# A hybrid decoder layer on one core: sums by another queue, weight tiles split in halves, the first keys' weights loaded early, small casts on VectorE

## The chip, the core and the metric

The kernel runs on one core of one Trainium2 chip. The metric is the device time of one execution in microseconds (us); less is better. TensorE (PE in the rows) does the matmuls, VectorE (DVE), ScalarE (ACT) and GpSimd (POOL) the rest, and SyncE (SP) issues most of the transfers between HBM and the on-chip memory. ScalarE and GpSimd have queues from which transfers are issued too.

## The reference

One layer over 576 tokens: a prompt of 512, and 8 sample sequences of 8 tokens with the same weights. All is float32.

```python
proj = x @ w_in                                   # u | q latent | kv latent | rotary key
y_ssm, h_last = s5_group(u, h0, p)                # complex diagonal scan, gelu, g * sigmoid(g @ w_glu)
q = (rms_norm(cq) @ w_uq); q_rope = rope(q[..., 128:])
q_lat = einsum(q[..., :128], w_uk)                # 8 heads; latent keys and values
o_lat = attend(q_lat, q_rope, ckv, krope)         # prompt: causal; sample: paged cache of 1024 + 8
y_att = einsum(o_lat, w_uv)
x = layer_norm(ALPHA*x + concat([y_ssm, y_att]) @ w_out)
x = layer_norm(ALPHA*x + (silu(x @ w_gate) * (x @ w_up)) @ w_down)
```

The model width is 2048, the feed-forward width 5632. The outputs are both `y`, the new kv latent and rotary key rows, and the last S5 states.

## The kernel before, in words

Every product keeps float32 accuracy by three matmuls: an operand is split into a high part `hi` (ScalarE copies it into the rounded type) and a low part `lo = raw - hi` (VectorE), and TensorE adds hi*hi, hi*lo and lo*hi. Weights are split on the chip too, so each weight tile costs a transfer, a ScalarE copy and a VectorE subtraction before TensorE can use all of it. Tokens go in two halves of 288 (`HALF`).

All engine instructions are recorded at one line (L181, the method that a planner's `Clock` wraps round every engine), so the tiles name the work: `wraw`, `whi`, `wlo` are a weight tile as it landed and its two parts; `mm` and `sc` are PSUM tiles; `xh/xl`, `Ah/Al`, `z`, `g`, `T` operands; `m` and `QS` also staging or sums.

The work is written as generators that yield until a time or a condition. `Layer.drive` and `merge` step them with the planner's estimated times (`nc.ready(tile)` is when it thinks a tile will be there), and the order in which they issue sets each engine's order, which a scheduler with priorities (`tc.cur_priority`) then refines. On the chip every engine runs its list in order and waits on semaphores.

The places that matter here:

- `Ring` holds a stream of weight tiles with two raw buffers and two split pairs. `dma` issues a load, `split` emits the ScalarE copy and the VectorE subtraction. `weights()` builds the ring of 1024 columns that serves `w_kv`, `w_uq`, `w_ukt`, `w_glu`, `w_out` and the first tiles of `w_gu`. The ring that serves `w_dn` in the feed-forward part has 1024 columns as well.
- `to_heads` ends the in-projection and starts the attention part. The wide tiles of the in-projection's weights (`wraw` 128x2048) and of the first queries' are freed there, and the ring's first two tiles, both halves of `w_kv[0]`, take their place.
- `queries`, `keys`, `qlats`, `values`, `score`, `attend` run head pairs of the prompt. `sides` runs beside them. GpSimd copies the sample tokens' columns of each query and of the latent into `qns`, `qrs` and `ckn` (40 small copies), and `sides` ends with transposes of `ckn` into `cnh`, `cnl`, for which it claims a PSUM tile twice.
- `gates` adds `g` halves on GpSimd (16 adds of 128x288).
- `ffn_phase` runs a seven-product (Strassen-like) form. `gate_up` leaves its results in HBM (`hd`), and the down product reads them back as 128x288 blocks. `ahead` lists the blocks, `loads` takes a free staging buffer (`xres` twice, `mraw`, `hraw`, and after `widen` seven pieces of `QS`, a tile that the last `gate_up` result is stored from), loads, copies to `hi`, subtracts to `lo`. `down` runs three chunks of the feed-forward width (c = 0, 1, 2). For each block of output columns it makes partial sums S (7 blocks of 288 columns, about 1 MB) that ScalarE evicts from PSUM into `m` (one buffer) or, in the last chunk, `m` and `QS` in turn; S leaves for HBM: `pa` in chunk 0 by SP's queue (8 stores), added onto `pa` by GpSimd's queue (10), `pb` by SP's queue (4, last chunk). `combine` reads them back.

The lines printed below are the functions that the diff touches.

Of the kernel before, what the change touches and what calls it, by code (L numbers as in the profile page):

```python
# [8 lines left out]
F32 = mybir.dt.float32  # L9
# [3 lines left out]
OP = mybir.AluOpType  # L13
# [6 lines left out]
TP = 512  # L20
# [318 lines left out]
class Ring:  # L339
# [31 lines left out]
    def split(self, j):  # L371
        while self.ns <= j < len(self.items):
# [12 lines left out]
            if self.split_fn:  # L385
                self.split_fn(hi, lo, raw, k)
            else:
                s = slice(0, math.prod(self.items[k].shape[1:]))
                tc = self.L.tc
                at = tc.cur_priority  # L390
                tc.cur_priority = at + 200
                self.L.split(hi[:, s], lo[:, s], raw[:, s])
                tc.cur_priority = at + 2
# [125 lines left out]
class Layer:  # L519
# [228 lines left out]
    def weights(self):  # L748
# [16 lines left out]
        for n in range(2 * HEADS):  # L765
            items += [io['w_gu'][n // 2, n % 2, 2 * r:2 * r + 2, :, :512].rearrange("q p c -> p q c") for r in range(2)]
        self.ring = Ring(self, self.wst, "w", 1024, items, ahead=100)

# [225 lines left out]
    def to_heads(self):  # L994

        nc = self.nc
        self.qns = self.mid2.tile([128, H, 2, TS], F32R, name="qns")
        self.qrs = self.mid2.tile([128, NB, 2, H, NS], F32R, name="qrs")
        self.QS = self.mid2.tile([128, 4, NB, H, NS], F32, name="QS")
        self.cn = (self.mid2.tile([64, 512], F32R, name="cnh"), self.mid2.tile([64, 512], F32R, name="cnl"))  # L1000
        self.ckn = self.mid2.tile([128, 4, 2, TS], F32R, name="ckn")
        self.QR, self.QN = {}, {}

        def main():
            w = yield from self.w_first.take()
            yield from self.rope_queries(0, *(x[:, 1024:] for x in w))
            yield from self.nope_queries(0, *w)

        self.mm_bufs = 4
        self.drive((main(), 1), *self.rest)  # L1010
        self.mm_bufs = 2
# [11 lines left out]
    def nope_queries(self, pr, wh, wl):  # L1023
        nc, p = self.nc, self.a0
        for hh in range(2):
# [11 lines left out]
            for i, x in enumerate((a, b)):  # L1037
                nc.gpsimd.tensor_copy(self.qns[:, h, i], x[:, TP:].bitcast(F32))
            self.QN[h] = (a, b)
# [9 lines left out]
            for i, x in enumerate((a, b)):  # L1049
                nc.gpsimd.tensor_copy(self.qrs[:, :, i, h],  # L1050
                                      x[:, TP:].rearrange("p (b s) -> p b s", b=NB).bitcast(F32))
# [416 lines left out]
    def prompt_phase(self):  # L1468
# [153 lines left out]
        def sides():  # L1622
# [4 lines left out]
            for i in range(4):  # L1627
                for j in range(2):
                    nc.gpsimd.tensor_copy(self.ckn[:, i, j], self.ckv[i][j][:, TP:].bitcast(F32))
            yield from qlats(0)  # L1630
            for pr in range(1, 4):
# [3 lines left out]
                yield from qlats(pr)  # L1635
                yield from values(pr)
            for j in range(2):
                ps = yield from self.claim()
                pt = ps[:64, 0]
                for i in range(4):  # L1640
                    nc.tensor.transpose(pt[:, i * 128:(i + 1) * 128], self.ckn[:, i, j].bitcast(F32), self.ident)
                nc.scalar.activation(self.cn[j], pt, AF.Copy)
                self.release(ps)
            done[0] = True
# [55 lines left out]
    def gates(self):  # L1700

        nc = self.nc
        for m in range(8):
# [3 lines left out]
            for hf in range(2):  # L1707
                nc.gpsimd.tensor_tensor(t[:, hf], g[0][hf].bitcast(F32), g[1][hf].bitcast(F32), OP.add)
            yield self.when(sg, t)
# [545 lines left out]
    def ffn_phase(self):  # L2255
# [38 lines left out]
        def loads(todo):  # L2294

            while True:
# [14 lines left out]
                nc.sync.dma_start(raw, src)  # L2311
                yield self.when(raw)
                nc.scalar.activation(hi, raw, AF.Copy)
# [73 lines left out]
        def down():  # L2387
            for c, n in enumerate(CHUNKS):
                for i in range(n2):
# [10 lines left out]
                    if c == len(CHUNKS) - 1 and i >= n2 // 2:  # L2400
                        nc.sync.dma_start(self.pb[i], S)
                    elif c:
                        nc.gpsimd.dma_start(self.pa[i], S, accum_op=OP.add)
                    else:
                        nc.sync.dma_start(self.pa[i], S)

# [100 lines left out]
```

## Time and profile before

| | |
|---|---|
| time, median of 3 runs | 2414.77 us (2414.47 to 2416.0) |
| the profiled execution: time | 2418.4 us |
| the profiled execution: span from first to last instruction | 2416.3 us |
| TensorE busy | 2316.1 us, 96% of the span, 17220 matmuls |
| VectorE busy | 1919.0 us, 79% |
| ScalarE busy | 1094.6 us, 45% |
| GpSimd busy | 48.8 us, 2% |
| mean granted TensorE clock | 0.982 |

The page gives busy time by engine. Since TensorE is busy nearly all the time, what counts is the rest: the stretches in which it waits and what ends each wait, and those in which its granted clock is below 1. A matmul of 288 columns starts every 0.13 us in a full stretch and every 0.24 us at the lower clock, so "busy" is longer than the work where the clock is down; the count of matmuls in a window of 20 us (150 or so in a full one) tells more.

### The profile page before, as it was taken

What the parts mean: (1) busy time and instruction counts of PE and PEld (TensorE: products, weight loads), DVE (VectorE), ACT (ScalarE), POOL (GpSimd) and SP (SyncE); (2) the same over time, 40 slices, a digit from 0 to 9 for tenths busy, and PEclk for the clock granted to TensorE, in tenths of its full rate; (3) what the DMA queues carried; (4) which work ended last, traced back from release to release, by engine and by line L of the source; (5) the groups of instructions that cost most, each with busy time, mean ns of one, the idle gap of its engine ahead of it and who ended that gap; (6) DMA issues with size and microseconds to landing.
All of it is one profiled execution on the core that took longest, in us unless ns stands there. A gap on an engine that the chain in (4) does not pass through costs nothing.

```text
span 2416.3 us, 44739 instructions
## 1 busy us (share of the span) xinstructions
PE 2316.1 (96%) x17220; PEld 2270.1 (94%) x17220; DVE 1919.0 (79%) x3465; ACT 1094.6 (45%) x1718; POOL 48.8 (2%) x93
## 2 busy tenths in 40 slices
PE   8999899999898999999999999999998999989996
PEld 8989799998798989999999999999998999989996
DVE  6898576778888896999988888887788776675878
ACT  4332565556555554333333333333335564464134
POOL 0000100110000000000000000000000000000000
PEclk9999899999999999999999999999999999999998
DMA  7663645678765565555433333332336665587722
GB/s 265 191 190 103 174 149 162 198 242 295 232 210 169 192 210 191 179 179 192 154 116 134 116 118 134 116 121 104 106 116 191 242 217 144 151 240 244 291 97 79
DMA packets 219352, 419.89 MB, mean 174 GB/s; under 512 B 62402, under 2 KB 127298, under 8 KB 217346
## 3 DMA queue, kind: packets, MB, share of 16 engines
q1 hardware_dynamic: 187346, 359.66, 44.8%
q10 hardware_dynamic: 30064, 44.98, 5.3%
q0 software_dynamic: 1728, 12.39, 2.8%
q8 instruction: 135, 2.21, 0.4%
q14 instruction: 79, 0.65, 0.1%
HBM read 337.52 MB, written 83.64 MB: 174 GB/s over the span
## 4 chain that ended last, share of the span: by engine, by line
PE 71%; DMA 11%; DVE 11%; ACT 4%; issue 3%; SPq 1%; ACTq 0%; DVEq 0%
PE mm L181 46%; PE sc L181 23%; DVE wlo L181 3%; DMA cktraw<-ckt 2%; ACT whi L181 1%; DMA xres<-hd 1%; PE po L181 1%; DMA wraw<-w_gu 1%; DMA wraw<-w_out 1%; DMA hd<-m 1%; DVE z L181 1%; DVE g L181 1%; DMA mraw<-so 1%; DVE E L181 1%; DVE QS L181 1%
## 5 line engine op out<-in xcount | busy, mean ns | idle before, releaser
L181 PE MATMUL mm<-xh,whi 128*128 128x288 f32 x2272 | 602.0, 301 | 18.7 <-ACT whi L181 8.8
L181 PE MATMUL mm<-xh,wlo 128*128 128x288 f32 x2272 | 602.0, 301 | 5.1 <-DVE wlo L181 4.9
L181 PE MATMUL mm<-xl,whi 128*128 128x288 f32 x2272 | 600.2, 300 | 0.9 <-DVE xl L181 0.9
L181 PEld LDWEIGHTS mm<-xh,whi 128*128 128x128 f32 x2272 | 404.7, 190 | 29.6 <-ACT whi L181 11.5
L181 PEld LDWEIGHTS mm<-xh,wlo 128*128 128x128 f32 x2272 | 404.8, 190 | 11.5 <-DVE wlo L181 8.5
L181 PEld LDWEIGHTS mm<-xl,whi 128*128 128x128 f32 x2272 | 404.9, 190 | 3.7 <-DVE xl L181 1.5
L181 PE MATMUL sc<-z,whi 128*128 128x288 f32 x1470 | 350.2, 297 | 0.0
L181 ACT ACTIVATE whi<-wraw 128x1024 fp32r<-128x1024 f32 (+2 forms) x159 | 174.0, 1095 | 276.6 <-PE mm L181 173.8
L181 ACT ACTIVATE whi<-E 128x1024 fp32r<-128x1024 f32 x120 | 127.1, 1059 | 331.4 <-issue 197.3
L181 DVE TENSOR_TENSOR wlo<-wraw,whi 128x1024 fp32r<-128x1024 f32 (+2 forms) x159 | 201.6, 1269 | 68.5 <-ACT whi L181 68.0
L181 PEld LDWEIGHTS sc<-z,whi 128*128 128x128 f32 x1470 | 250.8, 189 | 0.3 <-ACT whi L181 0.3
L181 ACT ACTIVATE whi<-rp 128x1024 fp32r<-128x1024 f32 x120 | 127.5, 1062 | 254.2 <-issue 195.2
L181 DVE TENSOR_TENSOR wlo<-E,whi 128x1024 fp32r<-128x1024 f32 x120 | 146.8, 1223 | 95.6 <-ACT whi L181 94.8
L181 PE MATMUL mm<-T,H 128*128 128x288 f32 x1200 | 216.1, 295 | 0.0
L181 DVE TENSOR_TENSOR wlo<-rp,whi 128x1024 fp32r<-128x1024 f32 x120 | 146.6, 1222 | 70.7 <-ACT whi L181 70.3
L181 PEld LDWEIGHTS mm<-T,H 128*128 128x128 f32 x1200 | 179.8, 188 | 0.0
L181 PE MATMUL sc<-Ah,H 128*128 128x288 f32 x552 | 145.4, 299 | 11.7 <-ACT m L181 9.9
L181 PE MATMUL sc<-g,whi 128*128 128x288 f32 x490 | 144.6, 295 | 2.1 <-ACT g L181 1.9
L181 PE MATMUL sc<-z,wlo 128*128 128x288 f32 x490 | 145.9, 298 | 0.5 <-DVE wlo L181 0.5
L181 PE MATMUL sc<-g,wlo 128*128 128x288 f32 x490 | 144.5, 295 | 0.0
L181 PE MATMUL mm<-Ah,H 128*128 128x288 f32 x552 | 144.2, 297 | 0.0
L181 PE MATMUL mm<-Ah,whi 128*128 128x288 f32 x480 | 134.0, 301 | 6.1 <-ACT whi L181 3.4
(488 smaller groups left out, 4930.3 us busy)
## 6 DMA issues: line engine op xcount, KB each, us to landing
wraw<-w_gu SPq DMA_DIRECT2D x145, 512.0 KB, 3.3
qns<-w_gu SPq DMA_DIRECT2D x59, 512.0 KB, 3.3
wraw<-w_out SPq DMA_DIRECT2D x56, 512.0 KB, 4.0
wraw<-w_dq SPq DMA_DIRECT2D x43, 512.0 KB, 4.4
cktraw<-ckt SPq DMA_DIRECT2D x64, 320.0 KB, 4.4
cknraw<-ckn SPq DMA_DIRECT2D x64, 256.0 KB, 4.3
hd<-QS ACTq DMA_DIRECT2D x16, 1008.0 KB, 6.3
wraw<-w_in SPq DMA_DIRECT2D x14, 1024.0 KB, 4.9
```

What stands on the lines that cost most here:

```text
L181: r = f(*a, **k)
```

## The change

Six things change:

- `Ring.split`: for a ring of 1024 columns, two copies and two subtractions of 512 columns each take the place of one of 1024.
- `to_heads` allocates the tile `QS` early (as `self.kv`, 128x2048), loads all of `w_kv[0]` into it in one transfer at a raised priority, and `weights` hands its halves to the ring as items 0 and 1. The real `QS` takes the buffer later, in `sides`.
- The 40 small copies and the 16 adds go from GpSimd to VectorE.
- `sides` claims one PSUM tile for both transposes of `ckn`, not two one after the other.
- `loads` of the feed-forward part plans the ScalarE copy of a block 1.5 us later than the planner's time of landing. This is no wait on the chip; it moves the copy, and what follows from it, in the order of the engines.
- `down` issues its `pa` and `pb` stores from ScalarE's queue; those that add onto `pa` stay on GpSimd's.

```diff
@@ Ring.split
-                self.L.split(hi[:, s], lo[:, s], raw[:, s])
+                n = s.stop // 2 if self.n == 1024 else s.stop
+                for i in range(0, s.stop, n):
+                    self.L.split(hi[:, i:i + n], lo[:, i:i + n], raw[:, i:i + n])
@@ weights
-        self.ring = Ring(self, self.wst, "w", 1024, items, ahead=100)
+        ring = self.ring = Ring(self, self.wst, "w", 1024, items, ahead=100)
+        ring.raw, ring.nd = {i: self.kv[:, 1024 * (1 - i):1024 * (2 - i)] for i in range(2)}, 2
@@ to_heads
-        self.QS = self.mid2.tile([128, 4, NB, H, NS], F32, name="QS")
+        self.kv = self.mid2.tile([128, 2048], F32, name="QS")
+        at = self.tc.cur_priority
+        self.tc.cur_priority = max(at - 400, 0)
+        nc.sync.dma_start(self.kv, self.io['w_kv'][0])
+        self.tc.cur_priority = at
@@ nope_queries, rope queries
-                nc.gpsimd.tensor_copy(self.qns[:, h, i], x[:, TP:].bitcast(F32))
+                nc.vector.tensor_copy(self.qns[:, h, i], x[:, TP:].bitcast(F32))
-                nc.gpsimd.tensor_copy(self.qrs[:, :, i, h],
+                nc.vector.tensor_copy(self.qrs[:, :, i, h],
@@ sides
-                    nc.gpsimd.tensor_copy(self.ckn[:, i, j], self.ckv[i][j][:, TP:].bitcast(F32))
+                    nc.vector.tensor_copy(self.ckn[:, i, j], self.ckv[i][j][:, TP:].bitcast(F32))
+            self.QS = self.mid2.tile([128, 4, NB, H, NS], F32, name="QS")
...
+            ps = yield from self.claim()
             for j in range(2):
-                ps = yield from self.claim()
-                pt = ps[:64, 0]
+                pt = ps[:64, j]
...
-                self.release(ps)
+            self.release(ps)
@@ gates
-                nc.gpsimd.tensor_tensor(t[:, hf], g[0][hf].bitcast(F32), g[1][hf].bitcast(F32), OP.add)
+                nc.vector.tensor_tensor(t[:, hf], g[0][hf].bitcast(F32), g[1][hf].bitcast(F32), OP.add)
@@ ffn_phase, loads
-                yield self.when(raw)
+                yield ('t', nc.ready(raw) + 1500)
@@ ffn_phase, down
-                        nc.sync.dma_start(self.pb[i], S)
+                        nc.scalar.dma_start(self.pb[i], S)
...
-                        nc.sync.dma_start(self.pa[i], S)
+                        nc.scalar.dma_start(self.pa[i], S)
```

**The start of the attention part, SP.** SP's transfers at the end of the in-projection before (`Sd<-hst` gathers S5 states, `U`, `M`, `P` belong to the S5 blocks):

```order
L181 DMA wraw<-w_uq 128x1536
L181 DMA Sd<-hst 64x8x63 x2
L181 DMA o_sp<-so 128x64
L181 DMA Sd<-hst 64x8x63 x13
L181 DMA wraw<-w_kv 128x1024 x2
L181 DMA Sd<-hst 64x8x63
L181 DMA U<-us_60 128x576
```

and now:

```order
L181 DMA wraw<-w_uq 128x1536
L181 DMA Sd<-hst 64x8x63 x2
L181 DMA o_sp<-so 128x64
L181 DMA Sd<-hst 64x8x63 x5
L181 DMA QS<-w_kv 128x2048
L181 DMA Sd<-hst 64x8x63 x5
L181 DMA wraw<-w_ukt 128x1024
L181 DMA wraw<-w_uq 128x512
L181 DMA Sd<-hst 64x8x63 x4
L181 DMA U<-us_60 128x576
```

The load of the first keys' weights stands ahead of nine of the state transfers that it stood behind, and two more weight loads stand before the last four.

**The same place, ScalarE**, before (`qnh`, `qrh`, `kr`, `rt` belong to the first queries and keys, `lsq` to a norm, `hst` to the S5 states):

```order
L181 ACTIVATE lsq<-mm 32x576 x4
L181 ACTIVATE hst<-S 128x1008
L181 ACTIVATE rt<-mm 32x576 x4
L181 ACTIVATE qnh<-mm 128x576
L181 ACTIVATE kr<-rva 128x576
L181 DMA o_kr<-rva 64x576
L181 ACTIVATE qnh<-mm 128x576
L181 ACTIVATE qrh<-qr 64x576 x4
L181 ACTIVATE whi<-wraw 128x1024 x2
```

and now:

```order
L181 ACTIVATE lsq<-mm 32x576 x4
L181 ACTIVATE qnh<-mm 128x576
L181 ACTIVATE rt<-mm 32x576 x4
L181 ACTIVATE hst<-S 128x1008
L181 ACTIVATE whi<-QS 128x512 x4
L181 ACTIVATE qnh<-mm 128x576
L181 ACTIVATE kr<-rva 128x576
L181 DMA o_kr<-rva 64x576
L181 ACTIVATE qrh<-qr 64x576 x4
```

The copies of the keys' weights, now four of 512 columns, stand ahead of one `qnh`, of `kr` and of the four `qrh`.

**The first blocks of the down product, ScalarE**, from the operand block `xh1` to the second eviction, before:

```order
L181 ACTIVATE xh1_193<-mraw_22285 128x288
L181 ACTIVATE xh1_193<-hraw_22292 128x288
L181 ACTIVATE T40_11236<-xres_22334 128x288
L181 ACTIVATE Ah4_10019<-xres_22340 128x288
L181 ACTIVATE Ah4_10019<-mraw_22343 128x288
L181 ACTIVATE whi_22206<-E_22198 128x1024
L181 ACTIVATE Ah12_5553<-hraw_22350 128x288
L181 DMA hd21_138<-QS_12323 128x1152
L181 ACTIVATE H_22202<-qns_22059 128x768
L181 ACTIVATE m_22196<-sc_22197 128x288
L181 ACTIVATE m_22196<-mm_22218 128x576
```

and now, from the first eviction on:

```order
L181 DMA hd21_138<-QS_12548 128x1152
L181 ACTIVATE H_22423<-qns_22284 128x768
L181 ACTIVATE m_22417<-sc_22418 128x288
L181 ACTIVATE xh6_198<-xres_22656 128x288
L181 ACTIVATE xh6_198<-xres_22659 128x288
L181 ACTIVATE xh3_195<-mraw_22824 128x288
L181 ACTIVATE xh1_193<-QS_22511 128x288 x2
L181 ACTIVATE z01_11811<-QS_22511 128x288 x2
L181 ACTIVATE g1_11720<-QS_22511 128x288
L181 ACTIVATE m_22417<-mm_22441 128x576
```

The block `xh1` comes now from pieces of `QS`, behind the store of `hd21` that reads `QS` and behind the first eviction, where it came from `mraw` and `hraw` ahead of both.

**The same place, TensorE**, before, from the products with `xh1`:

```order
L181 MATMUL mm_22218<-xh1_193,whi_22136 128x288
L181 MATMUL mm_22218<-xl1_209,whi_22136 128x288
L181 MATMUL mm_22218<-xh1_193,wlo_22137 128x288
L181 MATMUL mm_22218<-xh1_193,whi_22136 128x288
L181 MATMUL mm_22218<-xl1_209,whi_22136 128x288
L181 MATMUL mm_22218<-xh1_193,wlo_22137 128x288
L181 MATMUL mm_22265<-xh4_196,whi_22075 128x288
```

and now:

```order
L181 MATMUL mm_22482<-T40_11402,H_22296 128x288 x2
L181 MATMUL mm_22482<-T40_11402,H_22297 128x288
L181 MATMUL sc_22636<-Ah0_10040,H_22423 128x288
L181 MATMUL sc_22636<-Al0_10041,H_22423 128x288
L181 MATMUL sc_22636<-Ah0_10040,H_22424 128x288
L181 MATMUL sc_22636<-Ah0_10040,H_22423 128x288
L181 MATMUL sc_22636<-Al0_10041,H_22423 128x288
L181 MATMUL sc_22636<-Ah0_10040,H_22424 128x288
L181 MATMUL mm_22441<-xh1_193,whi_22359 128x288
L181 MATMUL sc_22456<-z01_11811,whi_22359 128x288
L181 MATMUL mm_22441<-xl1_209,whi_22359 128x288
```

The products with `xh1` stand now behind those of `xh4` and `T40` and behind the first product of the next output block (`sc_22636`); they stood ahead of all three.

## Rows read from the trace of the kernel before

**Rows 1.** The page, busy time, share and instructions of each engine.

```profile
PE 2316.1 (96%) x17220; PEld 2270.1 (94%) x17220; DVE 1919.0 (79%) x3465; ACT 1094.6 (45%) x1718; POOL 48.8 (2%) x93
```

**Rows 2.** TensorE's waits: engine, tile, releaser, us in total, times, longest.

```profile
PE mm L181 <- ACT whi L181: 23.0, 13, 10.8
PE sc L181 <- ACT m L181: 10.7, 6, 4.1
PE mm L181 <- DVE wlo L181: 8.6, 14, 1.1
```

**Rows 3.** TensorE, timeline at the first keys: start, us, instruction [idle before <-releaser].

```profile
281.08 0.58 PE L181 MATMUL mm<-whi,xh 128*128 128x256 f32 x1 [10.84 <-ACT whi L181]
282.65 0.79 PE L181 MATMUL mm<-xh,whi 128*128 128x512 f32 x1 [0.99 <-ACT whi L181]
```

**Rows 4.** SP's queue, timeline at the first keys.

```profile
258.67 15.01 SPq L181 DMA_DIRECT2D Sd<-hst  x13
273.78 1.13 SPq L181 DMA_DIRECT2D wraw<-w_kv  x2
```

**Rows 5.** ScalarE, timeline at the first keys.

```profile
266.77 2.61 ACT L181 ACTIVATE lsq<-mm 32x576 f32<-32x576 f32 x4
269.40 1.99 ACT L181 ACTIVATE hst<-S 128x1008 f32<-128x1008 f32 x1
...
274.05 0.65 ACT L181 ACTIVATE qnh<-mm 128x576 fp32r<-128x576 f32 x1
...
279.97 1.06 ACT L181 ACTIVATE whi<-wraw 128x1024 fp32r<-128x1024 f32 x1 [1.00 <-DMA wraw<-w_kv]
```

**Rows 6.** Weight splits by shape, ScalarE and VectorE: xcount | busy, mean ns | idle before.

```profile
L181 ACT ACTIVATE whi<-wraw 128x1024 fp32r<-128x1024 f32 x129 | 136.1, 1057 | 193.9 <-PE mm L181 105.5 <-DMA wraw<-w_gu 29.3 <-DMA wraw<-w_out 24.5
L181 ACT ACTIVATE whi<-wraw 128x512 fp32r<-128x512 f32 x15 | 9.5, 632 | 5.1 <-DMA wraw<-w_in 4.3 <-PE mm L181 0.6
...
L181 DVE TENSOR_TENSOR wlo<-wraw,whi 128x1024 fp32r<-128x1024 f32 x129 | 157.6, 1222 | 50.2 <-ACT whi L181 49.6
L181 DVE TENSOR_TENSOR wlo<-wraw,whi 128x512 fp32r<-128x512 f32 x15 | 10.2, 688 | 6.3 <-ACT whi L181 6.3
```

**Rows 7.** TensorE, timeline, two waits on one ring tile.

```profile
741.71 0.40 PE L181 MATMUL mm<-xh,whi 128*128 128x288 f32 x1 [1.06 <-ACT whi L181]
743.32 0.40 PE L181 MATMUL mm<-xh,wlo 128*128 128x288 f32 x1 [0.64 <-DVE wlo L181]
```

**Rows 8.** Windows of 20 us: busy time (instructions) of each engine, granted clock, DMA share, GB/s.

```profile
440.00:460.00 20.00, 17.65 (x119) 16.80 (x118) 16.66 (x42) 13.34 (x32) 0.00 (x0) 0.91 0.51 138
...
860.00:880.00 20.00, 16.53 (x116) 15.35 (x114) 20.00 (x31) 11.06 (x18) 0.00 (x0) 1.00 0.79 252
```

**Rows 9.** TensorE, timeline, the wait behind the transposes of `ckn`.

```profile
442.65 0.63 PE L181 MATMUL mm<-c,ckn 128*64 128x128 f32 x4 [2.35 <-ACT cnh L181]
```

**Rows 10.** VectorE, groups by shape: two like the added copies and adds.

```profile
L181 DVE TENSOR_TENSOR m<-m,sc 128x288 f32<-128x288 f32 x22 | 9.8, 448 | 0.0
L181 DVE TENSOR_TENSOR xl<-tmu,xh 128x64 fp32r<-128x64 f32 x8 | 1.4, 218 | 0.0
```

**Rows 11.** TensorE, timeline, waits in the down product.

```profile
1856.91 0.61 PE L181 MATMUL sc<-Ah,H 128*128 128x288 f32 x1 [4.05 <-ACT m L181]
...
1863.07 0.40 PE L181 MATMUL sc<-g,whi 128*128 128x288 f32 x1 [1.75 <-ACT g L181]
...
2173.00 0.40 PE L181 MATMUL sc<-Ah,H 128*128 128x288 f32 x1 [1.52 <-ACT H L181]
...
2247.28 0.40 PE L181 MATMUL mm<-xh,whi 128*128 128x288 f32 x1 [1.88 <-ACT whi L181]
```

**Rows 12.** ScalarE, timeline in the down product.

```profile
1860.32 0.94 ACT L181 ACTIVATE z<-QS 128x288 fp32r<-128x288 f32 x2 [0.89 <-DMA QS<-hd]
...
1870.63 0.63 ACT L181 ACTIVATE m<-mm 128x576 f32<-128x576 f32 x1
```

**Rows 13.** SP's queue, timeline in the down product.

```profile
1871.29 0.32 SPq L181 DMA_DIRECT2D pa<-m  x1
```

## The prediction, made before the changed kernel had run

> **What bounds the kernel now.** I read the page's busy shares first. TensorE is busy 2316.1 of 2416.3 us, and VectorE, the next, 1919.0 [rows 1]. So a change pays where TensorE waits or where its clock is down, and only there. The list of TensorE's waits comes next [rows 2]: 23.0 us in 13 waits for the high part of a weight tile, 8.6 us in 14 waits for the low part, 10.7 us in 6 waits for an eviction into `m`. The reader is to see that the biggest sum has one large member, 10.8 us. Then the timeline at each large wait, to see what was late, and the windows round it, to see what else was full.
>
> **The first keys.** TensorE stops at 270.24 (281.08 less 10.84) and starts at 281.08, does one matmul and waits 0.99 more before 282.65 [rows 3]. What is late is the transfer: SP issues thirteen `Sd<-hst` over 15.01 us and `w_kv` only at 273.78 [rows 4]; ScalarE copies it at 279.97 after 1.00 us of waiting for it [rows 5]. In the new order the load stands behind seven `Sd` transfers in all, two of them ahead of the stretch in the rows, so about a third into it, near 264; even if it takes twice what the two 0.5 MB loads took (273.78 to 279.97, 6.2 us), it lands at 276.4, and at the old pace near 270. ScalarE then decides. Its list ahead of the first copy is the four `lsq`, which end at 269.38, one `qnh`, the four `rt` and `hst`. The same work less one `qnh` and plus `kr` and a `qnh` ran before from 269.40 to 274.70 [rows 5], so the first new copy can start near 274.7 less 0.7, or 274.0. A copy of 512 columns takes 0.63, its subtraction 0.69 [rows 6]; TensorE now wants both, so it restarts at 275.4 at the earliest, and at 277 if VectorE's list or the landing is late. Idle time was 10.84 + 0.99 = 11.8 and is then 5.2 to 6.8, and no second wait follows, since three more copies of 0.63 keep ahead of 24 matmuls on each. The gain is 5.0 to 6.6; I take **5.5**, for the range 3 to 7 (3 if the transfer shares the engines badly). The `Sd` transfers that are passed, and the two loads put before the last four, delay the S5 blocks' state loads; the new order of TensorE has S5's products later too, which is the second rival's place.
>
> **Weight tiles in halves.** 129 tiles of 1024 columns are split at 1.057 us of ScalarE and 1.222 of VectorE; 15 of 512 columns at 0.632 and 0.688 [rows 6]. Where TensorE waits for a tile, the first half's high part is there 1.057 - 0.632 = 0.43 earlier, and its low part at 0.632 + 0.688 = 1.32 instead of 1.057 + 1.222 = 2.28, so 0.96 earlier. A typical tile cost 1.06 + 0.64 [rows 7] and should cost 0.6 and nothing. Outside the first keys the waits for high parts in rows 2 come to 23.0 - 11.8 = 11.2, less 1.9 at 2247.28 [rows 11], in about ten waits; 0.43 of each is 4. The low parts' 8.6 us in 14 waits average 0.6, less than 0.96, so most could go: 12.4 in all at the very best. But a tile that comes earlier lets TensorE run into the next one sooner, and where the transfer is what is late the next wait grows. I take **5**, range 0 to 10. The price is more instructions: 2 x 0.688 - 1.222 = 0.15 us of VectorE on each of 129 tiles, 20 us in all, and 0.21 on ScalarE, which has the room. VectorE is idle a fifth of the time, but not everywhere: from 860 to 880 it is busy 20.00 of 20 while TensorE has 116 matmuls [rows 8]. Five tiles in such a stretch cost 0.75. I take **-1**, range 0 to -5.
>
> **Copies and adds on VectorE.** 16 adds at 0.45 and 40 small copies at 0.22 [rows 10] are 16 us more of VectorE, spread over some 200 us in which it has a fifth free (16.66 of 20 in 440 to 460, [rows 8]). They free nobody: GpSimd is busy 2% [rows 1]. What hides them is VectorE's slack; if that cover is gone, up to a quarter of them, 4, shows. I take **-1**.
>
> **One claim for both transposes.** TensorE waits 2.35 us for `cnh` at 442.65, since the second claim needs the first's eviction [rows 9], and the clock of that window is 0.91 [rows 8]; 0.09 of 20 us is 1.8 more. With one claim the wait goes. But the attention's products come next, with little else between them. I take **2** of 4.2; range -4 to 4.2.
>
> **The down product.** The stores on ScalarE's queue: SP issued `pa` at 1871.29, right after the last eviction ended at 1871.26 [rows 12, 13], so the sum left at once before as well, and ScalarE's list cannot issue it earlier. An issue costs a queue 0.3 us [rows 13]; 12 of them on ScalarE, at 45%, cost nothing. What can be gained is that SP no longer stands at a store while loads queue behind it. The evictions' waits for a transfer out of `m` belong to the one buffer and to GpSimd's adds, which stay: nothing.
>
> The Trainium skill ("Trainium Kernel Development and Optimization", section Key Constraints) says that transfers issued from SyncE, ScalarE and GpSimd run on the same 16 engines and interleave, so that issuing from several saves only issue time. By that rule the move gains nothing but SP's freedom; without it the stores would stop delaying the loads, which is the third rival's time. The trace agrees in the 0.03 us between eviction and issue; it does not show a store on ScalarE's queue.
>
> The later plan for the blocks is not free in the first chunk. There TensorE waited 4.05 us at 1856.91 for an eviction that stood on ScalarE behind a block's copy, and 1.75 at 1863.07 for `g` [rows 11]. The first of these stays: a copy from `xres` and the store of `hd21` still stand ahead of the eviction. The products with `xh1` were done before it; now they need pieces of `QS`, which cannot be loaded before that store has read `QS`, and whose first two came at 1860.32 [rows 12]. So six matmuls (0.8 us) less stand ahead of the first wait, and TensorE has only the six of the next output block (1.4 us at the lower clock) between 1856.91 and the pieces at about 1861.3, and then `z01` and `g1` come piece by piece. By 1865 it has done some nine matmuls fewer, 1.2 to 2.2 us, and the clock stays down longer: **-3**, range 0 to -5. Against it stand waits that later blocks can spare: 1.52 at 2173.00 and 0.5 of the 1.88 at 2247.28 (a ring of halves) [rows 11], and about 1 in the small ones: **+3**, range 0 to 8. Together **0**, range -5 to 8.
>
> **The sum** is 5.5 + 5 - 1 - 1 + 2 + 0 = 10.5 us. The profiled execution took 2418.4, so a like one would take 2407.9; it stands 3.6 above the median of the runs shown, 2414.77, and against that the forecast is **2404.3**. With all gains at 7, 10, 4.2 and 8 and no costs it would be 2386; with the least gains and all costs (3, 0, -4, -5, -5, -4) 2430, which wants everything at its worst.
>
> **The rivals.** *Given back.* The gain at the first keys is only an earlier start, and the prompt's end gives it back: S5's last products come later in the new order, the scores and products of the last two heads have less work between them, and the wait at 442.65 returns elsewhere at 3 to 6 us; with the first chunk's 5 beside it the sum falls to 2 to 5 and the time is about 2411. For it: the clock of 0.91 and 119 matmuls in 440 to 460, a stretch already short of work [rows 8]. Against it: the long wait itself is cut by a transfer, not by an order.
>
> *VectorE becomes the bound.* 20 us of halves and 16 of copies and adds go onto an engine that in part of the ring's time is full. If it were on the path for all of them, they would cost 36 against gains of 12.5 and give 2438; from about 12.5 us, a third of them on the path, the change loses, and at half (18) the time is 2420. For it: 860 to 880 with 20.00 of 20 [rows 8]. Against it: the low parts wait only 8.6 us in all [rows 2], so elsewhere VectorE is ahead.
>
> *The down product gains what it is meant to.* If free loads and later copies take away all its waits, the 10.7 us for `m` [rows 2] and the 5.2 of the other rows 11, and some lower clock round them, it gives some 12 instead of 0: 2392. For it: waits there are for transfers. Against it: the largest is for an eviction whose cause stays.
>
> **How the numbers follow.** The forecast has a chance of 0.47 (2398 to 2409.9 its own range), given back 0.24 at 2411, VectorE 0.12 at 2420, the down product 0.17 at 2392. About 0.2% (4.8 us) is what a measurement of this kernel can tell from no change: 2409.9 and 2419.6. Faster are the forecast, the down product and a little of the given back: 0.66. The same: most of given back and a little of VectorE's: 0.22. Slower: 0.12. The range 2389 to 2418 leaves about 0.1 on either side.
>
> **What would show it.** At the first keys the wait falls from 10.84 to 5 to 7 and stands for `wlo`; if it is still 10, the load wasn't early or the copy stands behind something. Waits for `wlo` in rows 2 fall to under 4 us, and `whi`, first keys apart, to about 7. The wait at 442.65 is gone, and 440 to 460 has more than 119 matmuls; if fewer, it was given back. From 1850 to 1870 there are more idle microseconds than before, waits for `xh1`, `z01` or `g1`. 860 to 880 shows what the halves cost VectorE: fewer than 116 matmuls would speak for its rival. The prediction is wrong if the down product moves the time by more than 8 us either way, or if VectorE's added 36 us show as new waits for anything it makes.

## The result, and the profile after

The changed kernel takes 2430.55 us (median of 3 runs, 2430.02 to 2432.06), before 2414.77. The ratio is 1.0056, 95% interval 1.0040 to 1.0073: 14 us slower (the two medians alone stand 15.8 apart), where 10 us faster was forecast. The profiled execution took 2432.06 us, its span is 2430.3. In this text a saving or a cost in us from an experiment is its ratio to the kernel before, measured beside it on the same chip, times 2414.8, since the kernel before itself took 2418 to 2420 us there. Executions that were much longer at a far lower granted clock (the profiled one of `e10_late`: 0.75, where 0.98 is usual) are left out throughout.

The page's line on the engines and the longest of TensorE's waits (us in total, times, longest), after, to be held against [rows 1, 2]:

```profile
PE 2326.8 (96%) x17220; PEld 2278.4 (94%) x17220; DVE 1932.5 (80%) x3651; ACT 1109.4 (46%) x1852; POOL 13.9 (1%) x37
```

```profile
PE mm L181 <- ACT xh L181: 9.6, 4, 5.5
PE mm L181 <- DVE qnl L181: 8.6, 1, 8.6
PE mm L181 <- ACT whi L181: 8.3, 9, 3.3
PE sc L181 <- ACT m L181: 8.2, 3, 3.2
PE mm L181 <- DVE wlo L181: 6.5, 13, 2.9
PE sc L181 <- DVE olh L181: 5.5, 1, 5.5
...
PE sc L181 <- ACT e L181: 4.5, 5, 1.3
...
PE sc L181 <- DVE o L181: 2.7, 1, 2.7
```

The waits for weights fell, as forecast: `whi` from 23.0 to 8.3, `wlo` from 8.6 to 6.5. The waits for `xh` stood at 8.5 before too. But one wait of 8.6 stands at the first keys for something else, and three entries are new or nearly so: `e` and `olh` (neither in the list before) and `o` (0.2 before). To see what they cost, count matmuls by stage, since both kernels have the same 17220 and one takes 0.13 us in a full stretch. Windows (start:end, length, then busy time and instructions of PE, PEld, DVE, ACT, POOL, granted clock, DMA share, GB/s), before:

```profile
740.00:780.00 40.00, 32.96 (x222) 31.00 (x222) 32.11 (x70) 21.65 (x44) 0.00 (x0) 0.91 0.48 155
780.00:980.00 200.00, 192.41 (x1408) 189.08 (x1407) 162.97 (x263) 101.82 (x157) 0.00 (x0) 0.99 0.59 195
1840.00:1900.00 60.00, 52.56 (x358) 50.29 (x357) 50.94 (x94) 38.01 (x79) 0.00 (x0) 0.94 0.81 263
2240.00:2280.00 40.00, 37.58 (x266) 36.90 (x265) 35.13 (x57) 7.07 (x8) 0.00 (x0) 0.96 0.78 300
```

and after:

```profile
740.00:780.00 40.00, 31.53 (x178) 29.66 (x178) 26.22 (x63) 18.20 (x42) 0.00 (x0) 0.70 0.33 105
780.00:980.00 200.00, 191.65 (x1383) 186.99 (x1382) 164.66 (x307) 108.16 (x211) 0.00 (x0) 0.98 0.60 197
1840.00:1900.00 60.00, 50.40 (x330) 47.71 (x329) 49.93 (x94) 37.04 (x78) 0.00 (x0) 0.89 0.79 253
2240.00:2280.00 40.00, 35.55 (x251) 34.77 (x250) 25.60 (x44) 6.06 (x11) 0.00 (x0) 0.96 0.84 314
```

At 740 us the changed kernel is 25 matmuls ahead (3.3 us), as many as it wins from 260 to 300, at the first keys. From 740 to 980 it does 69 fewer (9.2 us), from 1840 to 1900 28 fewer (3.7 us), from 2240 to 2280 15 fewer (2.0 us); the other stages up to 2280 are within 11. Those three places are the loss.

The first of them is the end of the sample attention, a chain in which each link waits for the one before: the last product into `po`, its normalisation to `o` on VectorE, four transposes (`sc<-c,o`), an eviction into `QS`, the copy to `olh` on ScalarE, its low part on VectorE, and the products with `olh`. The timeline of the three engines, after:

```profile
744.21 0.39 PE L181 MATMUL po<-cnl,PT 64*128 64x512 f32 x1
...
747.30 1.12 PE L181 MATMUL sc<-c,o 128*128 128x128 f32 x4 [2.70 <-DVE o L181]
...
749.60 1.91 ACT L181 ACTIVATE olh<-QS 128x2048 fp32r<-128x2048 f32 x1
...
751.54 2.29 DVE L181 TENSOR_TENSOR olh<-QS,olh 128x2048 fp32r<-128x2048 f32 x1 [1.57 <-ACT olh L181]
...
753.89 0.47 PE L181 MATMUL sc<-olh,whi 128*128 128x128 f32 x1 [5.47 <-DVE olh L181]
```

and TensorE's before:

```profile
742.08 0.60 PE L181 MATMUL sc<-c,o 128*128 128x128 f32 x4
...
747.90 0.23 PE L181 MATMUL sc<-olh,whi 128*128 128x128 f32 x1
```

Before, the 5.2 us between transposes and products hold 24 matmuls of the in-between product (`mm<-xh`), and nine more stand ahead of the transposes. After, TensorE's order has nothing between the links, and it waits 2.70 and 5.47 us. I call the chain *covered* in the first case, *bare* in the second.

### The profile page after: what moved, and what is told of

It is laid out like the page before. It is cut to its first block, busy times and chain, and to the rows that moved or that the text cites. A ratio compares the mean times of both kernels' runs of the same rounds, so it can differ in the third digit from the quotient of the medians.

```text
span 2430.3 us, 44943 instructions
## 1 busy us (share of the span) xinstructions
PE 2326.8 (96%) x17220; PEld 2278.4 (94%) x17220; DVE 1932.5 (80%) x3651; ACT 1109.4 (46%) x1852; POOL 13.9 (1%) x37
## 4 chain that ended last, share of the span: by engine, by line
PE 64%; issue 13%; DMA 11%; DVE 9%; ACT 3%; SPq 0%; POOL 0%; ACTq 0%; DVEq 0%; POOLq 0%
PE mm L181 43%; PE sc L181 19%; DVE wlo L181 2%; DMA wraw<-w_gu 2%; PE po L181 1%; DVE z L181 1%; ACT whi L181 1%; DMA wraw<-w_dn 1%; DMA cktraw<-ckt 1%; DMA pa<-m 1%; DMA qns<-w_gu 1%; DMA qns<-w_dq 1%; DVE Al L181 1%; DVE g L181 1%; DVE xl L181 1%
## 5 line engine op out<-in xcount | busy, mean ns | idle before, releaser
L181 ACT ACTIVATE whi<-wraw 128x512 fp32r<-128x512 f32 (+2 forms) x287 | 184.4, 685 | 267.0 <-PE mm L181 166.2
L181 DVE TENSOR_TENSOR wlo<-wraw,whi 128x512 fp32r<-128x512 f32 (+2 forms) x287 | 210.9, 762 | 64.9 <-ACT whi L181 64.1
```

The lines of the kernel that those rows point to most:

```text
L181: r = f(*a, **k)
```

## The experiments

The theory A: the loss is the bare chain, plus the stores and the later plan in the down product. The rival B: the loss is the work put onto VectorE (halves, copies, adds; 36 us by the prediction's count).

**The two halves of the change apart.** `e1_front` is everything up to the down product, with the down product as before; `e2_down` the rest.

```diff
@@ e1_front, against after
-                yield ('t', nc.ready(raw) + 1500)
+                yield self.when(raw)
-                        nc.scalar.dma_start(self.pb[i], S)
+                        nc.sync.dma_start(self.pb[i], S)
...
@@ e2_down, against before
-                yield self.when(raw)
+                yield ('t', nc.ready(raw) + 1500)
-                        nc.sync.dma_start(self.pb[i], S)
+                        nc.scalar.dma_start(self.pb[i], S)
...
```

> The kernel before with the four edits of the attention part (early load of the first keys' weights, tiles in halves, copies and adds on VectorE, one claim), the down product as it was. Theory A (products spent early, and a bare chain of latencies at the end of the sample attention; the down product's own loss is separate): the 4.4 us of the down product's first chunk go, the waits for `o` and `olh` stay: 2424 to 2427. Theory B (VectorE's added load is the cause everywhere): 2425 to 2430, with waits for VectorE's tiles in many places. If the loss in the down product came only from arriving in another phase, nothing changes: 2430.

> The kernel before with only the later plan of the operand blocks and the stores on ScalarE's queue. Theory A: the loss in the first chunk stands by itself, waits for `xh1` and `z01` between 1855 and 1870: 2417 to 2420. Rival (the two edits are harmless and lose only beside the others): 2413 to 2416. Nothing up to 1840 us differs from before.

Measured: e1_front 1.0002 (0.9986 to 1.0019), no difference, where A had 2424 to 2427: the front is better than A said. e2_down 1.0028 (1.0013 to 1.0042), 6.8 us slower. So the change in the down product, which I had put at nothing, is a loss by itself.

**One part taken out.** `e3_no_halves` is after with whole weight tiles, `e4_no_late` after without the later plan.

```diff
@@ e3_no_halves, against after
-                n = s.stop // 2 if self.n == 1024 else s.stop
-                for i in range(0, s.stop, n):
-                    self.L.split(hi[:, i:i + n], lo[:, i:i + n], raw[:, i:i + n])
+                self.L.split(hi[:, s], lo[:, s], raw[:, s])
@@ e4_no_late, against after
-                yield ('t', nc.ready(raw) + 1500)
+                yield self.when(raw)
```

> The changed kernel with tiles of 1024 columns split in one piece again. Theory A: the products are spent early all the same, so the waits for `o` and `olh` stay; what goes is the price of the halves at 860 to 880 (2 us) and at the first tiles of `w_dn` (2 us), and what comes back are some waits for ring tiles: 2426 to 2431. Theory B: 20 us of VectorE go and with them most of the loss in the attention part: 2416 to 2422.

> The changed kernel with the operand blocks planned at their landing again, stores still on ScalarE's queue. If the later plan is what costs in the first chunk of the down product: 2425 to 2427, and the products with the second block stand ahead of the eviction again. If the stores on ScalarE's queue cost there: 2430.

Measured: e3_no_halves 1.0006 (0.9989 to 1.0023), where A had no gain and B had this. That doesn't show VectorE to be the cause yet, since without the halves the planner also covers the chain again (below). e4_no_late 1.0039 (1.0025 to 1.0054), some 4 us better than after, a difference that lies within the two intervals.

**One claim alone.** `e5_cn` is before with the one claim for both transposes.

```diff
@@ e5_cn, against before
+            ps = yield from self.claim()
             for j in range(2):
-                ps = yield from self.claim()
-                pt = ps[:64, 0]
+                pt = ps[:64, j]
...
-                self.release(ps)
+            self.release(ps)
```

> The kernel before with one claim for both transposes and nothing else. It adds no work to any engine, but in its order no product stands between the transposes of `o` and the products with `olh` at the end of the sample attention, where 33 stood. Theory A' (the order there, left bare, is what costs): waits for `o` and `olh` of 5 to 9 us in 735 to 755 appear, the wait for `cnh` at 443 goes, and the time is 2417 to 2421 on the scale on which before is 2414.8. Theory B (VectorE's added load costs): no such wait, 2411 to 2415.

Measured: 1.0021 (1.0009 to 1.0033), 5.1 us slower. TensorE's timeline:

```profile
444.77 0.63 PE L181 MATMUL mm<-c,ckn 128*64 128x128 f32 x4 [4.19 <-ACT cnh L181]
...
753.11 1.11 PE L181 MATMUL sc<-c,o 128*128 128x128 f32 x4 [2.92 <-DVE o L181]
759.27 0.47 PE L181 MATMUL sc<-olh,whi 128*128 128x128 f32 x1 [5.04 <-DVE olh L181]
```

The wait for `cnh` that the claim should take away (2.35 in [rows 9]) is 4.19, where it was expected gone; and these few lines make the chain bare, 300 us later.

**The chain, with and without the claim and VectorE's work.** `e6_kv_dve_halves` and `e12_kv_halves` are before with the early load and the halves, e6 also with the copies and adds on VectorE; `e7_kv_dve_cn` has the early load, the copies and adds and the claim; `e9_no_cn` is after with two claims again.

```diff
@@ e6, e7, e12, against before
+        ring.raw, ring.nd = {i: self.kv[:, 1024 * (1 - i):1024 * (2 - i)] for i in range(2)}, 2
+        nc.sync.dma_start(self.kv, self.io['w_kv'][0])
...
@@ e6, e12
+                for i in range(0, s.stop, n):
...
@@ e6, e7
-                nc.gpsimd.tensor_copy(self.qns[:, h, i], x[:, TP:].bitcast(F32))
+                nc.vector.tensor_copy(self.qns[:, h, i], x[:, TP:].bitcast(F32))
...
@@ e9_no_cn, against after (e7 has the opposite, against before)
-            ps = yield from self.claim()
             for j in range(2):
-                pt = ps[:64, j]
+                ps = yield from self.claim()
+                pt = ps[:64, 0]
```

> The kernel before with the early load, the copies and adds on VectorE and the halves: all the work that was added to VectorE and none of the other edits. In its order 33 products stand between `cnl` and `olh`, as before. Theory A': no waits for `o` or `olh`, the first keys' gain is kept to the end, 2404 to 2411. Theory B: the 36 us of VectorE show, 2417 to 2424.

> The kernel before with the early load, the copies and adds on VectorE and the one claim, tiles in one piece; the chain at the end of the sample attention is covered in its order. Theory A': 2407 to 2412, between the run with halves and before. Theory B: 2412 to 2416. Down product as before.

> The changed kernel with the two claims for the transposes again and nothing else undone. In its order 24 products stand ahead of the transposes of `o` and 24 between them and `olh`, where the changed kernel has none. If the bare chain is what cost the attention part: the waits of 2.7 and 5.5 us go, some 8 us with the lower clock behind them, and the time is 8 to 12 below the changed kernel, 2419 to 2423 on the scale on which before is 2414.8; what is left above before is the down product's. If the stores, the later plan and VectorE's load are enough by themselves: 2427 to 2431.

> The kernel before with the early load and the halves, the copies and adds left on GpSimd. Its order covers the chain at the end of the sample attention. Against the run that has them on VectorE as well: if these 16 us of VectorE cost about 1 us as forecast, it is 0 to 2 us faster than that one, 2403 to 2406 where that one is 2405; if GpSimd's slower copies hold somebody up, it is slower, 2407 to 2411.

Measured, on the scale on which before is 2414.8: e6 2405 and e7 2409, both as A' had them; e9 2415, better than the 2419 to 2423 expected; e12 2424, far above both of its values. The expectation of e12 says that its order covers the chain. That was a misreading: its order leaves it bare, as TensorE's timeline shows (and where e6's speaks of 33 products, its trace has 24 and 24):

```profile
749.47 1.11 PE L181 MATMUL sc<-c,o 128*128 128x128 f32 x4 [2.63 <-DVE o L181]
...
755.53 0.47 PE L181 MATMUL sc<-olh,whi 128*128 128x128 f32 x1 [4.95 <-DVE olh L181]
```

Read so, it is the case that was missing, bare with two claims. The kernels that differ ahead of the down product, with their order (how many products stand ahead of the transposes, and between them and the products with `olh`), sorted by what the windows from 740 to 980 count:

| kernel | claims | order | matmuls, 740 to 780 | 740 to 980 | ratio |
|---|---|---|---|---|---|
| e1_front | one | 0, 0 | 178 | 1553 | 1.0002 |
| after | one | 0, 0 | 178 | 1561 | 1.0056 |
| e12_kv_halves | two | 0, 0 | 172 | 1562 | 1.0038 (1.0025 to 1.0052) |
| e4_no_late | one | 0, 0 | 173 | 1573 | 1.0039 |
| e5_cn | one | 0, 0 | 184 | 1576 | 1.0021 |
| before | two | 9, 24 | 222 | 1630 | 1 |
| e3_no_halves | one | 9, 24 | 236 | 1635 | 1.0006 |
| e7_kv_dve_cn | one | 9, 24 | 232 | 1643 | 0.9978 (0.9965 to 0.9991) |
| e9_no_cn | two | 24, 24 | 231 | 1659 | 1.0001 (0.9989 to 1.0013) |
| e6_kv_dve_halves | two | 24, 24 | 237 | 1670 | 0.9961 (0.9948 to 0.9975) |

Every bare kernel does 1553 to 1576, every covered one 1630 to 1670, whether it claims once or twice. Before and the three kernels that share its order up to the down product (e2, e8, e11) count 1627 to 1632, so one execution differs from another by far less than this. With all the added work on VectorE (e6, e9) the count is highest. So the loss goes with the order, and B falls. Three pairs differ by the claim alone and have one bare and one covered chain: after against e9_no_cn, 0.0055 of ratio or 13 us, e1_front against e6, 0.0041 or 10 us, and e5_cn against before, 5 us, each with an uncertainty of 3 to 5 us. (e1_front is bare and yet no slower than before, since the other edits of the front gain about what its chain loses.) The same windows of e9_no_cn:

```profile
740.00:780.00 40.00, 36.04 (x231) 34.30 (x230) 34.54 (x83) 25.73 (x61) 0.00 (x0) 0.83 0.53 166
780.00:980.00 200.00, 193.79 (x1428) 190.19 (x1428) 169.98 (x313) 101.86 (x191) 0.00 (x0) 1.00 0.60 193
1840.00:1900.00 60.00, 48.99 (x309) 46.83 (x308) 43.34 (x81) 34.59 (x72) 0.00 (x0) 0.83 0.77 248
2240.00:2280.00 40.00, 35.84 (x249) 35.16 (x248) 34.55 (x60) 7.50 (x14) 0.00 (x0) 0.91 0.75 279
```

From 740 to 980 it does 98 more than after, 13.0 us at 0.133 each, as much as the whole difference. Of these, 53 (7 us) lie in the first 40 us, at the chain itself (waits of 8.2 us against 1.6, clock 0.70 against 0.83). Of the other 45, 29 lie from 860 to 900, at another place in the order. SP, after:

```profile
866.44 5.50 SPq L181 DMA_DIRECT2D hs<-xres  x2
872.04 0.39 SPq L181 DMA_DIRECT2D wraw<-w_gu  x1
```

A load of `w_gu` stands behind two stores of `hs`, and TensorE waits 3.25 us for the `whi` made from it. All four bare kernels with halves (after, e1, e4, e12) have this, with waits of 3.2 to 3.6; e6 and e9 have a single store there and waits of 1.25 and 1.34. So the pairs price the planner's order from 740 on, and the bare chain is about half of that; whether it brings on the second place isn't shown.

In the down product e9 loses as after does (49 and 17 fewer than before). The price of that part, from four pairs that differ by it alone: 6.8 us (e2 against before), 6.8 (e3 against e7), 9.7 (e9 against e6) and 13.0 (after against e1). e6, without the down part, is 9.4 us faster than before: it beats both kernels. So the 14 us are 9 won (e6), 10 lost with the claim (e1 against e6) and 13 lost with the down product's edits (after against e1).

**The down product's three edits.** `e10_late` is before with the later plan alone, `e8_pa_store` with the `pa` stores on ScalarE's queue, `e11_pb_store` with the `pb` stores there.

```diff
@@ e10_late, against before
-                yield self.when(raw)
+                yield ('t', nc.ready(raw) + 1500)
@@ e8_pa_store, against before
-                        nc.sync.dma_start(self.pa[i], S)
+                        nc.scalar.dma_start(self.pa[i], S)
@@ e11_pb_store, against before
-                        nc.sync.dma_start(self.pb[i], S)
+                        nc.scalar.dma_start(self.pb[i], S)
```

> The kernel before with the later plan of the operand blocks alone, stores on SP's queue. If the later plan costs by itself what was forecast in the first chunk (products with `xh1` behind the store of `hd21`): waits for `xh` and `z` of 1.5 us each at about 1861 and 1863 and 1 to 3 us in all up to 1900, nothing at 2240 to 2280: 2415 to 2418. If it costs only together with the stores: 2412 to 2415.

> The kernel before with only the eight `pa` stores of the first chunk on ScalarE's queue. If a store on a queue of its own shares the engines with the loads that it stood in line with before, it lands later and the next eviction into the one buffer `m` waits 2 to 4 us more, once or twice: 2417 to 2420. If the queue makes no difference: 2413 to 2416. The last chunk and the start of `w_dn` are as before.

> The kernel before with only the four `pb` stores of the last chunk on ScalarE's queue. If the last of them, on a queue of its own, shares the engines with the read of `pa` that it stood behind on SP's queue, that read lands some 2 us later, VectorE takes it up later and the first `wlo` of `w_dn` behind it: a wait for `wlo` of 2 to 3 us near 2250 where 0.5 stood, 2416 to 2419. If that wait came from the later plan: 2413 to 2416 and a wait of 0.5.

Measured: e10_late 1.0025 (1.0013 to 1.0038), 6.0 us, above both of its expected ranges. It has no usable profile; e2_down's TensorE shows the place:

```profile
1860.74 0.61 PE L181 MATMUL mm<-xh,whi 128*128 128x288 f32 x1 [1.54 <-ACT xh L181]
...
1862.98 0.61 PE L181 MATMUL sc<-z,whi 128*128 128x288 f32 x1 [1.63 <-ACT z L181]
...
1883.78 0.61 PE L181 MATMUL sc<-Ah,H 128*128 128x288 f32 x1 [3.36 <-ACT m L181]
```

The pair of waits for `xh` and `z` is in the four other kernels with the later plan (after, e2, e3, e9) and in none of the nine without it. From 1840 to 1900 those four do 309 to 340 matmuls, the nine 345 to 370.

e8_pa_store 1.0018 (1.0009 to 1.0028), 4.3 us. ScalarE waits for the store that must read `m` before the next eviction, in e8:

```profile
1872.97 0.33 ACTq L181 DMA_DIRECT2D pa<-m  x1
...
1879.21 1.01 ACT L181 ACTIVATE m<-sc 128x288 f32<-128x288 f32 x3 [2.33 <-DMA pa<-m]
...
1891.70 0.41 ACT L181 ACTIVATE m<-sc 128x288 f32<-128x288 f32 x1 [3.09 <-DMA pa<-m]
```

and before:

```profile
1877.80 1.01 ACT L181 ACTIVATE m<-sc 128x288 f32<-128x288 f32 x3 [1.70 <-DMA pa<-m]
```

The second of e8's waits has one of 0.22 as its counterpart before. The store leaves 0.98 us after its eviction has ended (1871.36 + 0.63), since two pairs of copies stand ahead of it in ScalarE's list; before, it left 0.03 after [rows 12, 13]. From 1840 to 1900, however, e8 does only 4 matmuls fewer than before (354), half a microsecond, and it was already behind by 1840, where its order is that of before. The execution shown is also the fastest of its twelve (2420.0 us, median 2423.4). How much of the 4.3 is the store is open.

e11_pb_store 1.0007 (0.9999 to 1.0016), 1.7 us, not told from nothing by its time, but its trace is plain. The timeline of SP's and ScalarE's queues, VectorE and TensorE in e11:

```profile
2235.40 0.33 SPq L181 DMA_DIRECT2D T<-pa  x1
...
2236.71 0.33 ACTq L181 DMA_DIRECT2D pb<-QS  x1
...
2246.35 2.83 DVE L181 TENSOR_TENSOR T<-T 128x576 f32<-128x576 f32 x4 [4.27 <-DMA T<-pa]
...
2252.56 0.85 PE L181 MATMUL mm<-xh,wlo 128*128 128x288 f32 x2 [2.97 <-DVE wlo L181]
```

and before:

```profile
2233.81 0.33 SPq L181 DMA_DIRECT2D T<-pa  x1
...
2235.10 0.33 SPq L181 DMA_DIRECT2D pb<-QS  x1
...
2242.39 2.83 DVE L181 TENSOR_TENSOR T<-T 128x576 f32<-128x576 f32 x4 [2.31 <-DMA T<-pa]
...
2248.61 0.53 PE L181 MATMUL mm<-xh,wlo 128*128 128x288 f32 x2 [0.53 <-DVE wlo L181]
```

The load of `T` is issued 1.3 us ahead of the store in both. It ends VectorE's wait 8.6 us after its issue with both on SP's queue, and 10.95 with the store on ScalarE's. VectorE makes `wlo` behind the adds of `T`, so TensorE waits 2.97 where it waited 0.53. All six kernels with the `pb` stores on ScalarE's queue (after, e2, e3, e4, e9, e11) have 10.4 to 10.95 there, a wait for `wlo` of 2.9 to 3.0, and 238 to 251 matmuls from 2240 to 2280; the seven others have 8.0 to 8.6, less than 0.6, and 264 to 291. So this cost is real, some 2 us.

How the price divides between plan and stores isn't settled. The three edits alone cost 6.0, 4.3 and 1.7, together 12, where e2_down with all of them costs 6.8; e4 against e1, which differ by the stores alone, gives 8.9.

## Why the prediction was wrong, step by step

**What failed first** was no term of the sum but a place without one, the end of the sample attention. I read the orders of both kernels at the first keys, at `cnh` and in the first chunk, and took the rest as moved by a little. The planner works with estimated times, so six edits shift its choices everywhere; it took the filling products out of the chain at 740 us. With that order 13 us are lost (after against e9; 10 and 5 in the two other pairs), some 7 of them at the chain itself, where a gain of 10.5 was forecast in all. It could have been read before any run: the orders alone show nine and 24 products between the links before, and none after (though I misread e12's and miscounted e6's). What makes the planner choose so isn't settled: one claim alone does it, e7 with one claim doesn't, e12 with two does.

**One claim, +2.** Failed. The wait for `cnh` is gone in after, but also in e9 with its two claims (0.53 there, for another tile), and it grew to 4.19 in e5. The end of it came with the other edits, not with the claim. In its place after has the five waits for `e`, 4.5 us from 408 to 443. 440 to 460 has 130 matmuls, as the sign wanted, but by 740 the kernel with one claim is 4 to 6 matmuls behind its partner with two in all three pairs (after and e9, e1 and e6, e5 and before): no gain.

**First keys, +5.5.** The mechanism was right, the size 3.3, at the lower end of 3 to 7. The timeline of SP, ScalarE, VectorE and TensorE after, against [rows 3 to 5]:

```profile
263.20 0.58 SPq L181 DMA_DIRECT2D QS<-w_kv  x1
...
276.07 2.17 ACT L181 ACTIVATE whi<-QS 128x512 fp32r<-128x512 f32 x4
276.72 2.50 DVE L181 TENSOR_TENSOR wlo<-QS,whi 128x512 fp32r<-128x512 f32 x4 [1.36 <-ACT whi L181]
...
278.27 0.65 ACT L181 ACTIVATE qnh<-mm 128x576 fp32r<-128x576 f32 x1
...
279.13 0.75 DVE L181 TENSOR_TENSOR qnl<-mm,qnh 128x576 fp32r<-128x576 f32 x1
...
279.94 0.58 PE L181 MATMUL mm<-whi,xh 128*128 128x256 f32 x1 [8.59 <-DVE qnl L181]
```

The first halves of the weights are split by 277.3 (276.72 and a quarter of 2.50), so TensorE could have started then, at the late end of my 275.4 to 277. It starts at 279.94, when `qnl` of the second query is done. The product with the keys doesn't read `qnl`; it writes a PSUM tile, and this eviction empties one (that reading rests on the releaser that the profile infers; no run put the eviction first, but in all eight kernels with the early load TensorE starts 0.05 or 0.06 us after that `qnl` ends). I had noted that the copies now stand ahead of that `qnh`, as a saving for the copies, and didn't ask who waits for the step that was passed. The idle time went from 11.8 to 8.6 instead of 5.2 to 6.8. By 740 the eight kernels with the early load have done 5242 to 5270 matmuls, the five without it 5221 to 5239, so the gain is kept until there.

**Halves, +5 and -1; copies, -1.** Not refuted, not isolated. e6 against e7 (halves and two claims, against whole tiles and one claim, both covered) gives 4 us, with intervals of 3 us on each, and e9 against e3, which differ in the same way, gives 1. The waits for `wlo` fell to 6.5, not under 4; without the longest, 2.9 in the down product, they are 3.6. The cost of the copies on VectorE wasn't told apart, since e12, which leaves them on GpSimd, has the other order. The price in VectorE's time was set too high: 36 us is a sum of durations, but instructions that follow each other overlap (two halves take 1.29 us together where one whole tile takes 1.22), and VectorE's busy time rose by 13.5, from 1919.0 to 1932.5.

**The down product, 0.** In the first chunk the step held and was too small: TensorE, after, against [rows 11]:

```profile
1863.09 0.61 PE L181 MATMUL sc<-Ah,H 128*128 128x288 f32 x1 [3.20 <-ACT m L181]
...
1867.07 0.61 PE L181 MATMUL mm<-xh,whi 128*128 128x288 f32 x1 [1.51 <-ACT xh L181]
1868.94 0.61 PE L181 MATMUL sc<-z,whi 128*128 128x288 f32 x1 [1.26 <-ACT z L181]
```

That is the wait for the eviction that stays, then the two for blocks that now come by `QS`. I took -3; the plan alone costs 6.0 in e10 (4 in after against e4), and the +3 from later blocks didn't come (from 1900 to 2240 after does 2471 matmuls, before 2472). Put at 0, range -5 to 8, the down product's edits cost 6.8 to 13.0. The stores, costed at nothing, are the second mis-sized term: the question "when does ScalarE issue it" was asked, and "which load did the old queue hold it behind" was not. The Trainium skill ("DMA: Bandwidth & Descriptors", section "Issuing engines are not separate DMA queues") says that transfers of all issuing engines run on the same 16 DMA engines and interleave, and that a second issuer saves only issue time. The traces agree, and show the other side of it: `T` lands 2.4 us later when the store that stood behind it on SP's queue comes from ScalarE's, as it would if the two interleave.

**The rivals.** *Given back* had the right kind of end in the wrong place: the gain at the first keys was kept to 740. For *VectorE becomes the bound* I had named a sign, fewer than 116 matmuls from 860 to 880. Only 97 came, and the rival is still wrong: e6 and e9, with the same work on VectorE, have 119 and 114 there. In after the stretch has a wait of 3.25 us for `whi` at 876.97 that e6 and e9 have at 1.25 and 1.34. The longest new waits, for `qnl`, `o` and `olh`, are all for tiles that VectorE makes, which was my other sign; but e5, which adds no work to any engine, has those for `o` and `olh` too. One sign can have two causes; only the experiments told them apart. *The down product gains what it is meant to* had the sign wrong: that part lost.

## What to carry to other kernels

When a scheduler sets the order, every edit moves all of it: before predicting, walk TensorE's order of both kernels along each serial chain (normalise, transpose, evict, split, multiply) and count the products between its links, because a wait of 8 us there costs more than many small gains. When a step is moved ahead of another, ask who waits for the one that was passed, its PSUM buffer included. A store that stood behind a load on one queue can delay that load when it is moved to another engine's queue: look for such a load before calling the move free.

## What the runs showed of the hardware

A load of `pa` landed 10.4 to 10.95 us after its issue instead of 8.0 to 8.6 when a store of about 1 MB that follows it by 0.8 to 1.3 us went out from another engine's queue (six kernels against seven). Instructions on VectorE that follow each other overlap: two subtractions of 512 columns took 1.29 us together, 0.69 alone. And a bare chain costs more than its waits: TensorE's granted clock from 740 to 780 was 0.70 with it, a mean of stretches at 1.2 and at 2.4 GHz (0.5 and 1), against 0.91 before, so that 178 matmuls, 44 fewer than before, kept it busy for 31.53 us where 222 had taken 32.96.
